# Two transformer blocks on one core: the first block's closing norm and the norm behind it from one pass of sums, and a feed-forward layer that starts before both

## The chip, the core and the metric

The kernel runs on one core of a Trainium2 chip. A core has five engines that run side by side, each through its own queue of instructions, in order, and that wait for one another on semaphores: PE (TensorE, matrix products into PSUM; the loading of its stationary operand is shown as PEld), DVE (VectorE), ACT (ScalarE), POOL (GpSimd, no access to PSUM) and SP, which here issues nearly all DMAs. The metric is the device time of one execution in microseconds.

## What is computed

The reference runs two stacked models on 256 tokens of width 1024, in float32. The first block ends with routed experts and a closing norm with the gain `g_final`; the second block takes that as its tokens `h`, beside a context `hc` of 256 tokens of its own, and begins with half of a feed-forward layer (FFN) on a norm that is scaled and shifted by a modulation.

```python
def first_block(...):
    ...
    x = x + _hier_moe(hm, ...).reshape(b, s, d)      # 32 experts, two per token
    return _rms_norm(x, g_final)                     # x / rms(x) * g_final

def _modulate(h, shift, scale):                      # rms norm without a gain, then scale and shift
    return _rms_norm_2(h) * (1.0 + scale) + shift

def second_block(x, c, ctx, ...):
    h, hc = x, ctx
    for layer in range(2):
        mod, modc = ...                              # from c and c_ctx: products with ada_w
        h = h + 0.5 * mod[:, 2] * _swiglu(_modulate(h, mod[:, 0], mod[:, 1]), ffn_w_in[layer, 0], ffn_w_out[layer, 0])
        hc = hc + ...                                # the same for the context
        ...                                          # a mixer, and a second FFN, for both
    return _rms_norm_2(h) * final_norm
```

## The kernel before

Activations lie feature-major: `xres` (the tokens) and `cres` (the context) are [128, 8, 256], eight chunks of 128 features by 256 tokens. Every fp32 product is made of three products of parts: a higher part `h` (a copy rounded by ACT to fp32r) and a lower part `l` (what is left, by DVE or POOL), for weights (`fsph`/`fspl` for tokens, `bsph`/`bspl` for the context, 128x512 each) and for activations (`fxh`/`fxl`, `bxh`/`bxl`). So 512 columns of weights are one ACT copy, one subtraction on DVE or POOL, and 12 matmuls with 256 columns.

Two streams are recorded: `fore` (names with f: first block, then the tokens of the second) and `back` (names with b: modulations and context). Within a stream each engine keeps the order in which the code emits; the two are merged by a priority (`seg`, a start and a slope), and a scheduler fixes one static order for each engine. Tile pools are small: three buffers each of `fsph`, `fspl`, `bsph`, `bspl` and of `fraw`, so a new part waits until PE is through with the part three before it. `Stream.low` chooses the engine of the lower parts: all of the context's go to POOL, the tokens' to DVE.

An FFN (`ffn_steps`) has 22 column blocks f: `gate_up(f)` makes the two products with 48 matmuls (gate and up), then tanh and products on ACT and DVE, and `down(r)` takes the finished blocks in rounds: 0 and 1, then four at a time.

`moe` (the routed experts) ends in a loop over left-over blocks; behind it comes the closing norm on the `fore` stream. `presum` squares the chunks (four ACT instructions 128x512) and adds them up on DVE (three adds 128x512, one 128x256); `stats` sums over features with matmuls by a column of ones; `newton` makes 1/rms on two columns with 12 small DVE instructions; `bcast` spreads it over all partitions (a DVE product with the identity, and a matmul by ones); eight DVE instructions then scale `xres` in place. `presum` runs again on the new `xres`, and `tokens()` begins with `modulated`, which is `stats`, `newton`, `bcast` and, per chunk, two DVE and one ACT instruction that make `fxh` and `fxl`. Only then the FFN's products can start. While this goes on, PE has matmuls of the context's FFN in its order.

The class `Ahead` is used by two later norms (layer 1): it splits g * res without the norm's factor (`step`), and the FFN's first two column blocks run on that, with the shift as two more columns (258 in place of 256). Meanwhile `factors` makes 1/rms; `norm` then makes the true `fxh` and `fxl` in the same place, `finish` completes the two early blocks, and the third block takes its weights in an order that follows the chunks. In these first blocks `EARLY_LOW` sends half of block 1's lower parts and all of block 2's to POOL. With `first`, four blocks instead of three come before `down(0)`, and one more ahead in the next round.

```python
            if f < early:                              # in gate_up, early = 2 with `first`
                p = [S.ps([128, 512])[:, :T + 2] for _ in range(2)]
            for s in range(2):
                self.proj_f(S, raw[s], KC, X, p[s])
                if f < early and s == 1 - f:
                    next(factors)
            ...
            if f == early - 1:
                first.norm()
                for i in range(early):
                    finish(i)
```

Of the kernel before, what the change touches and what calls it, by code (L numbers as in the profile page):

```python
# [15 lines left out]
OP = mybir.AluOpType  # L16
# [3 lines left out]
D = 1024  # L20
# [24 lines left out]
class Eng:  # L45
    """An engine whose instructions stay in the order in which the current chain emits them."""
# [23 lines left out]
class Stream:  # L70
# [11 lines left out]
    def seg(self, start, slope):  # L82
        """instructions from here on are due at start + slope * (matrix product time since here)"""
        self.start, self.slope, self.done = start, slope, 0.0
# [4 lines left out]
    def low(self, nc):  # L89
        """the engine of the next weights' lower parts"""  # L90
        self.lows += 1
        return nc.gpsimd if self.pool_low and self.lows % self.pool_low[1] < self.pool_low[0] else nc.vector
# [10 lines left out]
class Ahead:  # L103
    """a modulated norm whose reader starts without the norm's factors, on g * res and shift side by side"""
# [16 lines left out]
    def factors(self):  # L121
        """the factors token-major, and then what broadcasts them"""
# [9 lines left out]
    def norm(self):  # L132
        """the norm itself, in the same place"""
        nc = self.K.nc
        a = {}
        for c in range(KC + 1):
# [5 lines left out]
            if c > 0:  # L142
# [3 lines left out]
                                               op0=OP.add, op1=OP.subtract)  # L146


class Kern:
# [37 lines left out]
    def pair(self, S, src):  # L187
        """the two halves [128, 1024] of a unit"""
# [75 lines left out]
    def squares(self, S, res, d, one=False):  # L264
        """column blocks d and d + 1 of res are final: the squares for the norm that comes next, a step behind"""
# [18 lines left out]
    def presum(self, S, pairs):  # L284
        """the squares for the norm of what lies in pairs of chunks [128, 2, T]"""
# [33 lines left out]
    def head_rstd(self, S, y, eps):  # L319
        """1 / rms of each of the four chunks of y, as columns [128, (chunk, token block)]"""  # L320
# [22 lines left out]
    def gained(self, S, res, g, tag="k4"):  # L343
        """the parts of g * res, which lacks the norm's factors, and what makes those of one chunk"""
# [8 lines left out]
    def rstd_cols(self, S, st, n=D, eps=1e-6):  # L353
        """the norm's factors, token-major, from the sums of the squares"""
# [4 lines left out]
    def out_proj(self, S, src, X, res, gate, step=None):  # L359
        """res += gate * (X @ w), two column blocks per unit; step goes on with each final chunk"""  # L360
# [44 lines left out]
    def gated(self, S, src, n, out=None):  # L405
        """(tanh(src / 2) + 1) * src, twice the silu"""
# [12 lines left out]
    def ffn_steps(self, S, res, X, l, j, gate, first=None, then=None):  # L419
        """in steps of one round; first makes X, and then is what comes after it"""  # L420
# [8 lines left out]
        def product(f, a, b):  # L429
            """h = a * b"""  # L430
# [11 lines left out]
        def finish(f):  # L442
            """the rest of an early column block"""
# [84 lines left out]
    def ada(self, S, l, ms, tags):  # L528
        """the modulations ms of layer l, in steps of one load"""
# [24 lines left out]
    def logsig(self, S, z, shape):  # L554
        """log sigmoid of z, [128] + shape with 16 elements"""
# [23 lines left out]
    def narrow(self, S, src, n, m, tag="wg"):  # L579
        """the weights [128, KC * n] of n outputs, read in strips of m >= n columns"""  # L580
# [5 lines left out]
    def token_major(self, S, n, groups, passes):  # L586
        """the sums over the groups of k blocks, [128, 2, groups, n], of products with M = 128 / groups columns each"""
# [18 lines left out]
    def gates(self, S, w, n, X, bias, out, r=None):  # L606
        """out [128, 2, n] = r * (X @ w) + bias, token-major"""
# [7 lines left out]
    def doubled(self, S):  # L615
        """[128, 2, 72]: eight columns, and again from column 64 on"""
# [4 lines left out]
    def rows_hl(self, p, R):  # L621
        """the exact parts of eight rows: in R's rows 0 and 64 onwards"""
# [3 lines left out]
    def softmax(self, S, ps, nks, r=None):  # L626
        """softmax of the two query blocks of each p [128, 2, T], the first nks columns of which are keys;
        r are factors of the rows that p lacks"""
# [57 lines left out]
    def first_block(self, S):  # L686
# [37 lines left out]
        def queries(i):  # L724
            """keys and queries of a pair of heads: of the forgetting attention (i < 4) and of the differential one"""
# [17 lines left out]
        # forget gates  # L743
# [17 lines left out]
        # fox attention; keys and values of the memory  # L761
# [114 lines left out]
        # branches, gates and the output projection  # L876
# [40 lines left out]
        # cross attention  # L917
# [58 lines left out]
    def moe(self, S):  # L976
# [284 lines left out]
        if self.dbg:  # L1261
            self.dbg("x4", xres)
# [784 lines left out]
```

## Time and profile before

| | us |
|---|---|
| median of 3 runs | 2639.74 |
| lowest and highest run | 2637.49, 2642.59 |
| span of the profiled execution, first to last instruction | 2632.5 |
| PE busy in it | 2445.1 |

The profiled execution's own time is not listed beside its span; the median of the runs is 7.2 us above the span, and changes are worked out in the span and added to the median. A row that begins with a time is an instruction or a merged group: start, length, engine, line, operation, output and inputs, shapes, count, and in brackets the idle time just before it with what ended it.

### The profile page before, as it was taken

To read this page: it belongs to the slowest core of one execution; us is meant where nothing else is said; L and a number is where in the kernel's file an instruction comes from. 1 tells how busy PE (TensorE), PEld (TensorE's weight loads), DVE (VectorE), ACT (ScalarE), POOL (GpSimd) and SP (SyncE) were. 2 spreads that over 40 slices of the span, in tenths; PEclk is the share of its full clock that TensorE was granted. 3 is DMA by queue.
4 is the path that set the end of the run, shared out by engine and by line. 5 is a ranking of instruction groups with operands and counts; after the bars stand their busy time and mean duration, and the time that the engine had idled before them with its cause. 6 is when DMAs were issued, how large, how long until landed. Compare 5 with 4: busy or idle time off the path is not lost. (4 is left out here: it accounts for less than half of the span.)

```text
span 2632.5 us, 48460 instructions
## 1 busy us (share of the span) xinstructions
PE 2445.1 (93%) x19032; PEld 2073.7 (79%) x19032; DVE 1448.1 (55%) x3125; ACT 1186.9 (45%) x2342; POOL 730.4 (28%) x584
## 2 busy tenths in 40 slices
PE   6999998999988999999779999999999899888998
PEld 4767997785656787868359998876899899767998
DVE  6544767225433323332147676654766866676766
ACT  4433563334333433444125555543555555465554
POOL 1000145664424565656132004220100100333000
PEclk9999999999989999999779999999999999899999
DMA  9897443998988998989865553467555455312453
GB/s 346 325 317 247 171 142 112 357 329 296 364 317 336 350 347 296 366 324 345 321 250 175 186 189 125 164 202 269 195 175 182 154 184 185 112 65 97 161 186 119
DMA packets 117542, 617.37 MB, mean 235 GB/s; under 512 B 13488, under 2 KB 14960, under 8 KB 68288
## 3 DMA queue, kind: packets, MB, share of 16 engines
q1 hardware_dynamic: 115920, 610.20, 64.4%
q0 software_dynamic: 1392, 4.06, 0.5%
q8 instruction: 150, 2.46, 0.4%
q14 instruction: 80, 0.66, 0.1%
HBM read 612.11 MB, written 2.10 MB: 233 GB/s over the span
## 5 line engine op out<-in xcount | busy, mean ns | idle before, releaser
L58 POOL TENSOR_TENSOR bspl<-braw,bsph 128x512 fp32r<-128x512 f32 x468 | 608.9, 1308 | 947.6 <-ACT bsph L58 814.4
L58 ACT ACTIVATE fsph<-fraw 128x512 fp32r<-128x512 f32 x764 | 478.3, 628 | 540.3 <-PE fps L58 467.6
L58 DVE TENSOR_TENSOR fspl<-fraw,fsph 128x512 fp32r<-128x512 f32 x712 | 500.4, 706 | 309.2 <-ACT fsph L58 302.0
L58 PE MATMUL fps<-fxh,fspl 128*128 128x256 f32 (+1 forms) x2000 | 574.6, 287 | 3.9 <-POOL fspl L58 2.5
L58 PE MATMUL fps<-fxl,fsph 128*128 128x256 f32 (+1 forms) x2000 | 568.9, 284 | 8.8 <-DVE fxl L58 8.8
L58 PE MATMUL fps<-fxh,fsph 128*128 128x256 f32 (+1 forms) x2000 | 574.2, 287 | 3.1 <-ACT fsph L58 1.8
L58 ACT ACTIVATE bsph<-braw 128x512 fp32r<-128x512 f32 x468 | 291.7, 629 | 404.2 <-PE bps L58 350.4
L58 PEld LDWEIGHTS fps<-fxh,fspl 128*128 128x128 f32 x2000 | 381.8, 191 | 14.8 <-issue 5.8
L58 PEld LDWEIGHTS fps<-fxh,fsph 128*128 128x128 f32 x2000 | 383.3, 192 | 11.6 <-issue 4.8
L58 PEld LDWEIGHTS fps<-fxl,fsph 128*128 128x128 f32 x2000 | 382.7, 191 | 12.3 <-DVE fxl L58 11.3
L58 PE MATMUL bps<-bxh,bspl 128*128 128x256 f32 x1264 | 369.9, 293 | 2.1 <-ACT fk L58 2.1
L58 PE MATMUL bps<-bxh,bsph 128*128 128x256 f32 x1264 | 365.3, 289 | 5.5 <-ACT bsph L58 2.2
L58 PE MATMUL bps<-bxl,bsph 128*128 128x256 f32 x1264 | 362.4, 287 | 1.3 <-DVE bxl L58 1.3
L58 PE MATMUL fps<-fk,fsph 128*128 128x256 f32 x1632 | 299.3, 284 | 1.8 <-ACT fk L58 1.1
L58 PEld LDWEIGHTS bps<-bxh,bspl 128*128 128x128 f32 x1264 | 245.0, 194 | 53.1 <-POOL bspl L58 33.6
L58 PE MATMUL fps<-fraw,fk 128*32 128x512 f32 (+1 forms) x1600 | 234.9, 660 | 34.3 <-DMA fraw<-in_w_eu_dram 12.1
L58 PEld LDWEIGHTS bps<-bxh,bsph 128*128 128x128 f32 x1264 | 245.1, 194 | 26.5 <-issue 10.0
L58 PEld LDWEIGHTS fps<-fk,fsph 128*128 128x128 f32 x1632 | 254.8, 192 | 6.1 <-DVE fk L58 2.4
L58 PEld LDWEIGHTS bps<-bxl,bsph 128*128 128x128 f32 x1264 | 244.8, 194 | 17.6 <-issue 12.4
L58 POOL TENSOR_TENSOR fk<-fk,fk 128x512 f32<-128x512 f32 x16 | 21.6, 1349 | 761.9 <-ACT fk L58 756.8
L58 PE MATMUL fps<-fk,fspl 128*128 128x256 f32 x816 | 231.3, 283 | 0.0
L58 DVE SCALAR_TENSOR_TENSOR bk<-bk,bps 128x256 f32<-128x256 f32 (+1 forms) x148 | 60.5, 412 | 269.8 <-ACT bk L58 267.9
(353 smaller groups left out, 3482.3 us busy)
## 6 DMA issues: line engine op xcount, KB each, us to landing
fraw<-in_ffn_in_dram SPq DMA_DIRECT2D x88, 1024.0 KB, 4.9
braw<-in_ffn_in_dram SPq DMA_DIRECT2D x132, 512.0 KB, 6.2
fraw<-in_w_eg_dram SPq DMA_DIRECT2D x66, 1024.0 KB, 7.5
fraw<-in_w_eu_dram SPq DMA_DIRECT2D x66, 1024.0 KB, 7.3
fraw<-in_w_ed_dram SPq DMA_DIRECT2D x66, 1024.0 KB, 7.5
braw<-in_ada_w_dram SPq DMA_DIRECT2D x91, 512.0 KB, 6.1
fraw<-in_ffn_out_dram SPq DMA_DIRECT2D x44, 1024.0 KB, 4.9
braw<-in_ffn_out_dram SPq DMA_DIRECT2D x66, 512.0 KB, 5.6
```

Of the source, the lines that this page charges most:

```text
L58: r = f(*args, **kw)
```

## The change

`moe` no longer scales `xres` behind the loop. It makes the higher and lower parts of `xres * (g_final * scale)`, eight chunks, adds up the squares of `xres` as before, and a second sum of the squares of `g_final * xres` (eight ACT squares 128x256, the adds on POOL). The first FFN of the tokens takes the new `Ahead2` as `first`. From the two sums `factors` works out r1 (of the closing norm), then r of the norm behind it, with two Newton iterations one after the other, and two broadcasts. `norm` also scales `xres` itself, with eight DVE instructions behind the sixteen of the norm. What the diff leaves out are removed comments and docstrings.

```diff
+class Ahead2(Ahead):
+    def __init__(self, K, S, S2, res, g1, scale, shift):
+        super().__init__(K, S, S2, res, S.t("c", [128, KC]), shift)
+        self.g1, self.scale, self.all = g1, scale, res
+
+    def step(self, c):
+        if c == 0:
+            self.K.nc.vector.tensor_tensor(self.g, self.g1, self.scale, op=OP.mult)
+        super().step(c)
+
+    def factors(self):
+        K, S, nc = self.K, self.S, self.K.nc
+        st = self.S2.ps([128, 512])
+        for i, sq in enumerate(self.sq):
+            for b in range(2):
+                K.mm(st[:, 2 * i + b:2 * i + b + 1], sq[:, b * 128:(b + 1) * 128], K.ones[:, 0:1], True, True)
+        r1 = S.t("gc", [128, 2])
+        nc.vector.tensor_copy(r1, K.newton(S, st[:, 0:2], 2, 1.0 / D, 1e-6))
+        s2 = S.t("c", [128, 2])
+        nc.vector.tensor_tensor(s2, r1, r1, op=OP.mult)
+        nc.vector.tensor_tensor(s2, s2, st[:, 2:4], op=OP.mult)
+        r = K.newton(S, s2, 2, 1.0 / D, 1e-6)
+        nc.vector.tensor_tensor(r, r, r1, op=OP.mult)
+        yield
+        p = self.S2.ps([128, 512])
+        K.bcast(S, r, 2, p[:, :T])
+        K.bcast(S, r1, 2, p[:, T:])
+        self.bc = S.t("q1", [128, T])
+        self.b1 = S.t("q1", [128, T])
+        nc.scalar.activation(self.bc, p[:, :T], AF.Copy)
+        nc.scalar.activation(self.b1, p[:, T:], AF.Copy)
+        yield
+
+    def norm(self):
+        super().norm()
+        for c in range(KC):
+            self.K.nc.vector.scalar_tensor_tensor(self.res[c], self.res[c], self.g1[:, c:c + 1], self.b1,
+                                                  op0=OP.mult, op1=OP.mult)
...
         pairs = [xres[:, c:c + 2] for c in range(0, KC, 2)]
+        g4 = self.gains[:, 4]
+        a = self.first_ahead
+        for c in range(KC):
+            a.step(c)
         self.presum(S, pairs)
-        bc = self.rstd_bcast(S, [xres[:, c] for c in range(KC)], 1e-6)
-        for c in range(KC):
-            nc.vector.scalar_tensor_tensor(xres[:, c], xres[:, c], self.gains[:, 4, c:c + 1], bc,
-                                           op0=OP.mult, op1=OP.mult)
-        self.presum(S, pairs)
...
+        plain = S.sq[0]
+        gained = None
+        for c in range(0, KC, 2):
+            sq = S.t("k2", [128, 2, T])
+            for i in range(2):
+                nc.scalar.activation(sq[:, i], xres[:, c + i], AF.Square, scale=g4[:, c + i:c + i + 1])
+            if gained is None:
+                gained = sq
+            else:
+                nc.gpsimd.tensor_tensor(gained, gained, sq, op=OP.add)
+        nc.gpsimd.tensor_tensor(gained[:, 0], gained[:, 0], gained[:, 1], op=OP.add)
+        S.sq = None
+        a.sq = (plain, gained[:, 0])
...
         x = K.xres
-        X = K.modulated(fore, x, 0, 0, 0)
-        for _ in K.ffn_steps(fore, x, X, 0, 0, K.mods_col(0, 2, 0)):
+        for _ in K.ffn_steps(fore, x, None, 0, 0, K.mods_col(0, 2, 0), first=K.first_ahead):
             yield
...
     fore.seg(*SEG["route"])
+    K.first_ahead = Ahead2(K, fore, back, K.xres, K.gains[:, 4], K.mods_col(0, 1, 0), K.mods_col(0, 0, 0))
     K.moe(fore)
```

Until the end of the loop every engine's order is the same in both kernels. Behind it, ACT had these rows before (`fk<-xres` are the squares, `bsph` the context's weights, `fsph` the first weights of the tokens' FFN):

```order
L58 ACTIVATE fk_14238<-xres 128x512
L58 ACTIVATE fk_14241<-xres 128x512
L58 ACTIVATE fk_14244<-xres 128x512
L58 ACTIVATE bsph_14343<-braw_14292 128x512
L58 ACTIVATE bsph_14372<-braw_14367 128x512
L58 ACTIVATE bsph_14388<-braw_14367 128x512
L58 ACTIVATE fsph_14807<-fraw_14804 128x512
```

And it has these now, behind the copy of the shift:

```order
L58 ACTIVATE bsph_14339<-braw_14288 128x512
L58 ACTIVATE fxh_14238<-xres,fc_12036 128x256 x8
L58 ACTIVATE fk_14258<-xres 128x512
L58 ACTIVATE fk_14260<-xres 128x512
L58 ACTIVATE fk_14263<-xres 128x512
L58 ACTIVATE fk_14266<-xres 128x512
L58 ACTIVATE bsph_14368<-braw_14363 128x512
L58 ACTIVATE bsph_14384<-braw_14363 128x512
L58 ACTIVATE fsph_14748<-fraw_14744 128x512
L58 ACTIVATE fsph_14764<-fraw_14744 128x512
```

The eight chunks now stand ahead of the context's next weights and of `fsph_14748`. In PE's order 19 matmuls of the context lead, then two that read `bsph_14368`, then the first two of column block 0, which read `fsph_14748`; before, the sum of the squares followed the first nine, and block 0 came some 240 matmuls of the context later. All of block 0 now stands in front of those; the sums of the squares stand behind them, then half of block 1, then 22 of the context's, then the two broadcasts, then the rest of block 1.

On DVE, the end of the second Newton iteration and its broadcast read so before (`fc` are its columns, `fk<-consts` makes the broadcast's operand, `cres` is the context's update):

```order
L58 TENSOR_TENSOR fc_14753<-fc_14753,fc_14751 128x2
L58 SCALAR_TENSOR_TENSOR fc_14752<-fc_14753,fc_14752 128x2
L58 TENSOR_TENSOR fk_14767<-consts,fc_14752 128x256
L58 SCALAR_TENSOR_TENSOR bk_14593<-bk_14591,bps_14526 128x256
L58 SCALAR_TENSOR_TENSOR bk_14595<-bk_14593,bps_14526 128x256
L58 TENSOR_TENSOR bk_14597<-bk_14595,bk_14597 128x256
```

And so now:

```order
L58 TENSOR_TENSOR fc_14839<-fc_14839,fc_14837 128x2
L58 SCALAR_TENSOR_TENSOR cres<-bps_14713,mods,cres 128x256 x2
L58 SCALAR_TENSOR_TENSOR fc_14838<-fc_14839,fc_14838 128x2
L58 SCALAR_TENSOR_TENSOR fc_14839<-fc_14838 128x2
L58 TENSOR_TENSOR fc_14839<-fc_14839,fc_14837 128x2
L58 SCALAR_TENSOR_TENSOR fc_14838<-fc_14839,fc_14838 128x2
L58 TENSOR_TENSOR fc_14838<-fc_14838,fgc_14817 128x2
L58 TENSOR_TENSOR fk_14890<-consts,fc_14838 128x256
L58 TENSOR_TENSOR fk_14893<-consts,fgc_14817 128x256
```

The context's update stands inside the iteration, and what it reads, `bps_14713`, is finished by the last of the 22 matmuls that stand right in front of the broadcasts on PE.

Behind the norm DVE's order is now this (`xres<-xres,gains,fq` scales the residual, `fspl_15101` belongs to column block 3, the rest is `finish` of block 0); before, there was no such row between the norm and the next lower parts:

```order
L58 SCALAR_TENSOR_TENSOR xres<-xres,gains,fq_14897 128x256 x8
L58 TENSOR_SCALAR fc_14972<-fps_14746 128x1
L58 COPY fc_14972<-fps_14747 128x1
L58 SCALAR_TENSOR_TENSOR fk_14973<-fps_14746,fq_14896 128x256
L58 TENSOR_TENSOR fspl_15101<-fraw_15081,fsph_15100 128x512
L58 TENSOR_TENSOR fspl_15117<-fraw_15081,fsph_15116 128x512
```

The eight scalings stand ahead of the lower parts that block 3 needs. From the end of block 3 on PE's order is that of before (one column block fewer stands in the next round), up to the tokens' even mixer; from there to the next layer's first FFN the scheduler placed some of the context's matmuls and two loads of `ada_w` a little earlier.

## Rows read from the trace of the kernel before

**Rows 1.** The page: span, busy time, and PE's busy share and granted clock in 40 slices.
```profile
span 2632.5 us, 48460 instructions
PE 2445.1 (93%) x19032; PEld 2073.7 (79%) x19032; DVE 1448.1 (55%) x3125; ACT 1186.9 (45%) x2342; POOL 730.4 (28%) x584
...
PE   6999998999988999999779999999999899888998
...
PEclk9999999999989999999779999999999999899999
```
**Rows 2.** Stretches of time behind the loop: busy us of each engine, granted clock, DMA.
```profile
1350.50:1400.40 49.90, 43.14 (x303) 42.27 (x303) 42.85 (x81) 26.89 (x53) 30.31 (x23) 0.86 0.52 180
1400.40:1420.00 19.60, 19.60 (x166) 19.60 (x166) 14.25 (x30) 10.56 (x21) 2.44 (x2) 1.00 0.63 219
1420.00:1580.00 160.00, 160.00 (x1353) 160.00 (x1352) 112.16 (x210) 84.86 (x152) 0.00 (x0) 1.00 0.53 187
```
**Rows 3.** PE in order of time: all its waits between 1350 and 1400 us.
```profile
1352.62 0.39 PE L58 MATMUL bps<-bxh,bspl 128*128 128x256 f32 x1 [2.09 <-ACT fk L58]
...
1355.80 1.01 PE L58 MATMUL fps<-consts,fk 128*128 128x1 f32 x4 [1.66 <-DVE fk L58]
...
1367.11 0.70 PE L58 MATMUL fps<-fk,consts 128*128 128x256 f32 x2 [0.82 <-DVE fk L58]
...
1378.61 0.95 PE L58 MATMUL fps<-consts,fk 128*128 128x1 f32 x4 [2.19 <-DVE fk L58]
```
**Rows 4.** Stretches of 1 us where the granted clock (third from the end) changes.
```profile
1354.00:1355.00 1.00, 0.14 (x2) 0.00 (x0) 0.97 (x2) 0.62 (x2) 1.00 (x1) 0.91 1.11 467
...
1360.00:1361.00 1.00, 1.00 (x7) 1.00 (x6) 1.00 (x2) 0.00 (x0) 1.00 (x1) 0.50 1.03 422
1361.00:1362.00 1.00, 1.00 (x8) 1.00 (x7) 1.00 (x5) 0.41 (x1) 0.14 (x1) 0.68 1.01 414
...
1378.00:1379.00 1.00, 0.39 (x3) 0.39 (x3) 0.89 (x3) 0.08 (x1) 0.00 (x0) 0.86 0.44 111
...
1385.00:1386.00 1.00, 1.00 (x8) 1.00 (x8) 0.70 (x2) 0.24 (x1) 0.96 (x1) 0.73 0.71 225
```
**Rows 5.** ACT in order of time, behind the loop and at a later norm of this kind.
```profile
1350.87 2.19 ACT L58 ACTIVATE fk<-xres 128x512 f32<-128x512 f32 x4 [7.14 <-PEq L1245]
1352.97 1.66 ACT L58 ACTIVATE bsph<-braw 128x512 fp32r<-128x512 f32 x3
...
2055.57 0.91 ACT L58 ACTIVATE fxh<-xres,mods 128x256 fp32r<-128x256 f32 x2
```
**Rows 6.** POOL, and DVE's small instructions of a Newton iteration beside it, in order of time.
```profile
1382.49 1.27 POOL L58 TENSOR_TENSOR bspl<-braw,bsph 128x512 fp32r<-128x512 f32 x1 [1.28 <-ACT bsph L58]
...
1382.25 0.16 DVE L58 SCALAR_TENSOR_TENSOR fc<-fc,fc 128x2 f32<-128x2 f32 x1
1382.45 0.16 DVE L58 SCALAR_TENSOR_TENSOR fc<-fc 128x2 f32<-128x2 f32 x1
1382.64 1.14 DVE L58 TENSOR_TENSOR fc<-fc,fc 128x2 f32<-128x2 f32 x1
```
**Rows 7.** PE in order of time at the later norm: sum of squares, and broadcast.
```profile
2070.34 0.50 PE L58 MATMUL bps<-consts,fk 128*128 128x1 f32 x4
...
2076.31 0.70 PE L58 MATMUL bps<-fk,consts 128*128 128x256 f32 x2 [2.46 <-DVE fk L58]
```
**Rows 8.** The stretch from that broadcast until the early blocks are finished.
```profile
2076.30:2100.00 23.70, 20.00 (x148) 18.50 (x149) 20.25 (x43) 13.88 (x30) 4.32 (x3) 1.00 0.35 125
```
**Rows 9.** DVE in order of time: the scaling of xres, and an update of the context.
```profile
1367.84 3.23 DVE L58 SCALAR_TENSOR_TENSOR xres<-xres,gains,fps 128x256 f32<-128x256 f32 x8 [0.46 <-PE fps L58]
...
1388.61 0.86 DVE L58 SCALAR_TENSOR_TENSOR cres<-bps,mods,cres 128x256 f32<-128x256 f32 x2
```
**Rows 10.** PE's waits from 1400 us to the end: total us, times, longest.
```profile
PE bps L58 <- DMA braw<-in_ada_w_dram: 13.0, 10, 2.3
```

More of the change, by code (lines that the diff above doesn't have):

```diff
@@ L1254, in moe @@
         pairs = [xres[:, c:c + 2] for c in range(0, KC, 2)]
+        g4 = self.gains[:, 4]
+        a = self.first_ahead
+        for c in range(KC):
+            a.step(c)
         self.presum(S, pairs)
-        bc = self.rstd_bcast(S, [xres[:, c] for c in range(KC)], 1e-6)
-        for c in range(KC):
-            nc.vector.scalar_tensor_tensor(xres[:, c], xres[:, c], self.gains[:, 4, c:c + 1], bc,
-                                           op0=OP.mult, op1=OP.mult)
-        self.presum(S, pairs)
-        if self.dbg:
-            self.dbg("x4", xres)
+        plain = S.sq[0]
[11 more added lines that the diff above has]
+        a.sq = (plain, gained[:, 0])
     def conv_silu(self, S, p, n, scale, out):
```

## The prediction

> **What bounds the kernel now.** The page comes first: PE is busy 2445.1 of 2632.5 us and its slices read 9 nearly everywhere, except at the start, in slices 20 and 21 (about 1250 to 1380 us), where the granted clock falls too, and in some later slices [rows 1]. The change works at the end of that dip, so I went on to stretches of time. From 1350.5 us, the end of the expert loop, to 1400.4 us PE is busy 43.14 of 49.90 us; behind that it is busy all the time until 1580 us [rows 2]. So whatever PE loses between 1350.5 and 1400.4 is lost for good, and whatever the change wins or loses there should reach the end as it is.
>
> PE loses in two ways there. The first is idle time, 49.90 - 43.14 = 6.76 us, and PE's own list shows it all: 2.09 us at the loop's exit, 1.66 before the first sum of squares, 0.82 before the first broadcast, 2.19 before the second sum [rows 3]. The rest of both norms is already covered by the context's matmuls. The second is the clock: it falls to 0.5 (1.2 GHz) late in the microsecond from 1354 and is back at 1361.7, and again from 1378.9 to 1385.6 [rows 4]; at full clock PE starts 1353 matmuls in 160 us, one every 0.118 us [rows 2], and at half the clock each takes twice that. PE is at work in some 5.8 us of the first stretch and 6.7 of the second, and half of that is lost: 6.2 us. Together 13.0 us, of which 2.1, the exit, stays in any case.
>
> **What the change does to PE's own work.** Almost nothing. There are two sums of squares and two broadcasts as before; 96 matmuls get 258 columns in place of 256, 96 x 0.118 x 2/256 = 0.1 us. Column block 3 only changes places with the first round's `down`. Everything hangs on waits. I lay the new order out from the loop's exit, with durations from the rows, and add up what PE loses until the end of block 3.
>
> **First wait: the chunks stand ahead of the weights on ACT.** ACT begins at 1350.87. The copy of the shift is small (0.3 as an estimate, below the 0.4 of a chunk); one 128x512 copy takes 0.52 (1.66 for three, whose last tail is 0.1), a scaled chunk 0.41 (0.91 for two), four squares 2.1 [rows 5]. So `bsph_14368` is ready at 1350.87 + 0.3 + 0.52 + 8 x 0.41 + 2.1 + 0.6 = 1357.7, and `fsph_14748` one copy later and one more, at about 1358.75. PE starts at 1352.62 as before [rows 3], has 19 matmuls (2.3 us) and then must wait from 1354.9, with 0.25 us of work on the way: **3.6 us**. It is 2.5 if a chunk takes only half of a square, 0.27 (8 x 0.14 = 1.1 less), and 3.9 if the first chunk waits 0.3 for DVE's product of the two gains.
>
> **POOL and DVE behind it.** Four adds for the second sum (3 x 1.3 and 0.7 us) now stand on POOL between the context's lower parts, 1.27 us each. Rows 6 show what that does to DVE: an instruction of 0.16 us that starts while POOL is at work takes 1.14 us and ends when POOL ends. DVE has the adds of squares, `fspl_14749` and the context's products there, and ACT's `fsph_14796` stands behind a copy that waits for such a product. It costs nothing if DVE slips between, and one and a half POOL instructions, 2.0, if not; I take **0.9**.
>
> **The clock.** PE is idle for 2.1 us, works for 2.3 and is idle again for 3.6. Before, 4.4 us with 1.4 of work came ahead of the first fall, and an idle time of 2.19 us ahead of the second [rows 3, 4]. A fall costs at most what it did, 3.3; none costs 0. I take **2.5**, nearer to the fall, since the idle time is longer here than at either place.
>
> Up to here (block 0 and some 45 of the context's matmuls) PE has lost 9.1 us, where it lost 2.1 + 1.66 + 0.82 + 2.9 = 7.5 before. From there the context's matmuls run without the wait of 2.19 and the fall of 3.3.
>
> **Second wait: the factors.** The sums stand some 190 matmuls later. Behind them PE has 24 matmuls of block 1 and 22 of the context's, 5.5 us, then the broadcasts. DVE needs 13 small instructions (0.195 from start to start) [rows 6], two products, 13 more, one product and the operand of the broadcast (0.43). Inside stands the update of `cres`, which needs the last of PE's 22 matmuls; so, however fast DVE is, PE waits for 0.3 us until that product has landed, 0.86 for the update [rows 9], four small instructions and a product (1.0) and 0.43: at least 2.5 us. At most: the five POOL subtractions that fall into this stretch each hold an instruction back by 1.0 us, as in rows 6, and a sixth the broadcast's, so that the chain ends 12.0 us behind the sums and PE waits 5.8. The nearest row, one iteration at the later norm, took 5.97 us from sum to broadcast, and PE waited 2.46 with 24 fewer small steps to wait for [rows 7]. I take the middle, **4.2**.
>
> Here the Trainium skill bears on the sum: its page "SBUF — State Buffer", section "Who interferes with whom", says that a DVE instruction with two SBUF inputs and a GpSimd instruction that reads SBUF exclude each other for the whole instruction, and that the order of issue decides who blocks. Our rows show such waits, 1.14 for 0.16 us, but not at every overlap: the row at 1382.45 has one input and runs on. Taken as strictly as the page states it, this wait would be 5.8 and the whole sum 1.6 us more than mine.
>
> **Third wait: the norm, and the scaling of xres.** From the broadcast on the program is that of the later norm, where PE lost 23.70 - 20.00 = 3.7 us until the early blocks were finished [rows 8]; I take **3.7**, between 2.9 (without the longest POOL delay) and 4.5. New is the scaling of `xres` on DVE between the norm and block 3's lower parts and `finish`: 3.23 us [rows 9]. At the later norm PE already waits there, so little is left to hide it: 0 if it is hidden, 3.2 if not, taken **2.7**. A second fall of the clock, behind the wait for the factors, would cost block 1's last 24 matmuls 2.3 us, mostly hidden by the norm: **0.3**.
>
> **The sum.** After: 2.1 + 3.6 + 0.9 + 2.5 + 4.2 + 3.7 + 2.7 + 0.3 = 20.0 us lost, before 13.0: **7.0 us more**. All lower ends give 10.0 (3.0 us less), all upper ones 27.1 (14.1 more). SP's queue has the same DMAs; one load of the tokens moves ahead of four of the context's, whose buffers come free later anyway. The span would be 2639.5 us, the median 2639.7 + 7.0 = **2646.7 us**. 0.2% is 5.3 us, about what this measurement can tell from no change.
>
> **The rivals.**
> 1. *Waits of the same size, no change.* DVE slips between POOL's instructions and the clock holds: 2.1 + 3.6 + 0.2 + 0.5 + 2.6 + 3.7 + 1.2 = 13.9, 0.9 more, 2640.6 us. For it: the second iteration of before took 4.3 us in spite of POOL, and the later norm had no fall. Against it: 3.6 us of idle time at the first wait is fixed by ACT's order, and the five POOL instructions by PE's.
> 2. *DVE is held at each step.* The factors take 12 us, the clock falls twice, `xres` is not hidden: 5.8 + 3.2 + 2.3 and the other upper ends, 10 to 14 more, about 2651.5 us. For it: rows 6. Against it: what the norm hides.
> 3. *Not slower, by the loads of `ada_w`.* PE waits 13.0 us in ten pieces for these loads further on, the longest 2.3 [rows 10]. Two of them now stand earlier. If each takes one such wait with it, 4.6 are won: 2.4 more remain, 2642.1 us, no change; from one wait (1.7 us) on the result is inside 0.2%, and it takes six of them for a gain. Against it: loads that stand earlier only shift the wait where the DMA queue is the bound.
>
> **Chances.** The forecast (3 to 10 more) 0.45; rival 1 0.28; rival 2 0.15; rival 3 0.12. Slower by over 0.2%: two thirds of the forecast's and all of rival 2, 0.46. Within 0.2%: the rest of the forecast, most of rivals 1 and 3, 0.41. Faster: the ends of rivals 1 and 3, in which the order further on wins several us, 0.13. The range leaves out 1 in 10 on either side: from 4.0 us less (all lower ends and 1 us further on) to 15.3 more (all upper ends and 1): 2636 to 2655. The forecast's own is 2642.7 to 2649.7.
>
> **What would show it.** Right: PE idle for about 3 us and then 0.8 us before its first 258-column matmul, near 1355 to 1359; no waits of PE from there to the sums near 1394; an idle time of 2.5 to 6 us in front of the broadcasts; column block 3 with a wait for `fspl` of about 2 us, and its end near 1427 instead of 1420. Wrong: if the clock stays at 1.0 from 1350 to 1430, or the broadcasts wait below 2 us, the loss shrinks to rival 1; if PE shows the same loss up to block 3 and the end comes elsewhere, the order further on decided it.

## The result: 0.64% slower

| | before | changed |
|---|---|---|
| median, us | 2637.07 (7 runs, 2629.24 to 2642.59) | 2652.28 (7 runs, 2643.78 to 2657.14) |
| span of the profiled execution | 2632.5 | 2650.5 |
| ratio to before, 95% interval | | 1.0064 (1.0045 to 1.0083) |

The forecast was slower, 2646.7 us, with a range up to 2655; the time lies in the range and on the forecast's side, 5.6 us above its likeliest value. The change itself is larger than that sounds: the forecast added 7.0 us to a median of three runs (2639.74), and with seven runs the median of before is 2637.07, so the medians are 15.2 us apart, twice the forecast and as much as its upper end (15.3). The ratio's interval is 12 to 22 us.

The page of the changed kernel has the same dip in slices 20 to 22 (compare [rows 1]):

```profile
span 2650.5 us, 48502 instructions
...
PE 2457.1 (93%) x19032; PEld 2077.4 (78%) x19032; DVE 1450.2 (55%) x3137; ACT 1192.1 (45%) x2359; POOL 742.1 (28%) x594
...
PE   6999998999989999999778999999999999888998
...
PEclk9999999999999999999689999999999999899999
```

Both kernels have 19032 matmuls, so stretches of equal work can be cut by counting them. I cut one from PE's first matmul behind the loop (to within 0.2 us of its start) over 635 matmuls (column blocks 0 to 3 and the context's work between them lie in it) and one over the next 1181. A row gives the ends and the length, the busy time of PE, PEld, DVE, ACT and POOL, then the granted clock, the DMA share and GB/s. Of before:

```profile
1352.62:1440.02 87.40, 82.73 (x635) 81.89 (x636) 70.67 (x136) 46.80 (x90) 32.76 (x24) 0.92 0.54 192
1440.02:1580.07 140.05, 140.05 (x1183) 140.05 (x1182) 98.10 (x183) 73.76 (x132) 0.00 (x0) 1.00 0.54 188
```

And of the changed kernel, with the rest of the span as a third row:

```profile
1353.36:1452.97 99.61, 85.78 (x636) 82.41 (x637) 73.45 (x146) 52.94 (x106) 44.92 (x34) 0.93 0.47 168
1452.97:1594.42 141.45, 141.45 (x1183) 141.45 (x1182) 98.40 (x183) 73.71 (x133) 0.00 (x0) 1.00 0.53 186
1594.42:2650.50 1056.08, 982.77 (x7726) 907.46 (x7725) 715.49 (x1487) 540.13 (x1058) 161.97 (x131) 0.96 0.46 160
```

The 18.0 us between the two spans are 0.7 that were there before the change's first instruction (1353.36 - 1352.62), **12.2 in the stretch of the change** (99.61 - 87.40), **1.4 in the next**, in which PE is never idle in either kernel, and 3.7 behind it. In the first stretch PE is idle for 99.61 - 85.78 = 13.8 us in place of 4.7; the low clock takes as much of it as before (0.93 of 99.61 and 0.92 of 87.40 are both some 14 us at half the clock). PE's waits there over 0.15 us, in order of time, with the sums (1395.66) among them:

```profile
1353.29 0.39 PE L58 MATMUL bps<-bxh,bspl 128*128 128x256 f32 x1 [2.15 <-ACT fxh L58]
...
1358.06 0.39 PE L58 MATMUL bps<-bxh,bsph 128*128 128x256 f32 x1 [2.25 <-ACT bsph L58]
...
1359.10 0.58 PE L58 MATMUL fps<-fxh,fsph 128*128 128x258 f32 x1 [0.54 <-ACT fsph L58]
...
1363.08 0.39 PE L58 MATMUL fps<-fxh,fspl 128*128 128x258 f32 x1 [0.78 <-DVE fspl L58]
...
1369.02 0.39 PE L58 MATMUL fps<-fxh,fsph 128*128 128x258 f32 x1 [1.08 <-ACT fsph L58]
...
1370.48 0.39 PE L58 MATMUL fps<-fxh,fspl 128*128 128x258 f32 x1 [0.36 <-DVE fspl L58]
...
1395.66 0.95 PE L58 MATMUL bps<-consts,fk 128*128 128x1 f32 x8
...
1407.70 2.08 PE L58 MATMUL bps<-fk,consts 128*128 128x256 f32 x4 [5.50 <-DVE fk L58]
...
1418.00 0.39 PE L58 MATMUL fps<-fxh,fsph 128*128 128x256 f32 x1 [0.17 <-ACT fsph L58]
...
1419.65 0.39 PE L58 MATMUL fps<-fxh,fspl 128*128 128x256 f32 x1 [1.14 <-POOL fspl L58]
...
1424.65 0.36 PE L58 MATMUL fps<-fxh,fsph 128*128 128x256 f32 x1 [0.97 <-DVE fk L58]
...
1431.81 0.88 PE L58 MATMUL fps<-fk,fsph 128*128 128x256 f32 x2 [0.84 <-ACT fk L58]
```

The 2.19 us in front of the second sum are gone (the row at 1395.66 has no wait), and 5.50 stand before the broadcasts in their place. Most waits also cost something that is no idle time: the first matmul behind one takes 0.39 us and not 0.28, and the next starts as much later.

What DVE did between the sums and the broadcasts, with POOL beside it:

```profile
1396.25 1.28 POOL L58 TENSOR_TENSOR bspl<-braw,bsph 128x512 fp32r<-128x512 f32 x1
...
1398.77 2.75 POOL L58 TENSOR_TENSOR fspl<-fraw,fsph 128x512 fp32r<-128x512 f32 x2 [1.24 <-ACT fsph L58]
1401.47 2.68 POOL L58 TENSOR_TENSOR bspl<-braw,bsph 128x512 fp32r<-128x512 f32 x2
...
1396.64 0.16 DVE L58 TENSOR_SCALAR fc<-bps 128x2 f32<-128x2 f32 x1 [0.15 <-PE bps L58]
1396.84 0.72 DVE L58 TENSOR_SCALAR fc<-fc 128x2 int32<-128x2 int32 x1
...
1398.97 1.14 DVE L58 SCALAR_TENSOR_TENSOR fc<-fc 128x2 f32<-128x2 f32 x1
...
1400.34 1.20 DVE L58 SCALAR_TENSOR_TENSOR fc<-fc,fc 128x2 f32<-128x2 f32 x1
1401.57 1.22 DVE L58 COPY fgc<-fc 128x2 f32<-128x2 f32 x1
...
1403.21 0.95 DVE L58 TENSOR_SCALAR fc<-fc 128x2 f32<-128x2 f32 x1
...
1407.57 0.42 DVE L58 TENSOR_TENSOR fk<-consts,fgc 128x256 f32<-128x256 f32 x1
```

The line from the first small instruction to the second operand takes 11.4 us. Five instructions in it that take 0.16 to 0.17 elsewhere last 0.72 to 1.22, each until a POOL instruction is done; together that is 4.4 us. Two of the five are `TENSOR_SCALAR` and one a `COPY`, with one input each. Behind the broadcasts the clock is low as well, although PE works without a break: the rows are two stretches of the changed kernel at half the clock.

```profile
1408.00:1413.00 5.00, 5.00 (x20) 4.64 (x20) 2.53 (x6) 2.39 (x6) 0.11 (x1) 0.50 0.00 0
1420.00:1423.00 3.00, 3.00 (x17) 3.00 (x16) 3.00 (x8) 0.00 (x0) 0.00 (x0) 0.50 0.71 243
```

### The profile page after: what moved, and what is told of

Its sections match the earlier page's. It is cut to its first block, busy times and chain, and to the rows that moved or that the text cites. A ratio compares the mean times of both kernels' runs of the same rounds, so it can differ in the third digit from the quotient of the medians.

```text
span 2650.5 us, 48502 instructions
## 1 busy us (share of the span) xinstructions
PE 2457.1 (93%) x19032; PEld 2077.4 (78%) x19032; DVE 1450.2 (55%) x3137; ACT 1192.1 (45%) x2359; POOL 742.1 (28%) x594
## 5 line engine op out<-in xcount | busy, mean ns | idle before, releaser
L58 PEld LDWEIGHTS fps<-fxh,fsph 128*128 128x128 f32 x2000 | 386.8, 193 | 13.8 <-issue 5.0
```

What stands on the lines that cost most here:

```text
L58: r = f(*args, **kw)
```

## The experiments

All are measured against the kernel before. The first three columns of numbers behind the ratio are of the same 635 matmuls as above, the last of the 1181 behind them; each is one profiled execution. In it the low clock comes and goes with the execution (0.90 to 0.96 in these stretches), so idle time tells more than length.

| kernel | ratio (95% interval) | stretch, us | PE idle | granted clock | next 1181 matmuls, us |
|---|---|---|---|---|---|
| before | | 87.40 | 4.7 | 0.92 | 140.05 |
| changed | 1.0064 (1.0045 to 1.0083) | 99.61 | 13.8 | 0.93 | 141.45 |
| 1 sums in the tokens' PSUM | 1.0068 (1.0052 to 1.0085) | 98.64 | 12.3 | 0.91 | 141.45 |
| 2 xres scaled later | 1.0075 (1.0060 to 1.0089) | 100.12 | 14.2 | 0.93 | 141.46 |
| 3 both | 1.0051 (1.0038 to 1.0064) | 96.51 | 13.3 | 0.96 | 141.45 |
| 4 the tokens' work off POOL | 1.0056 (1.0037 to 1.0076) | 95.98 | 12.0 | 0.95 | 141.46 |
| 5 shared sums alone | 1.0072 (1.0051 to 1.0093) | 101.11 | 15.3 | 0.90 | 140.04 |
| 6 early start alone | 1.0021 (1.0005 to 1.0037) | 92.54 | 10.2 | 0.96 | 141.45 |
| 7 changed, chunks 256 apart | 1.0071 (1.0049 to 1.0092) | 100.62 | 16.0 | 0.95 | 140.04 |
| 8 before, chunks 256 apart | 0.9997 (0.9979 to 1.0015) | 85.97 | 4.7 | 0.94 | 140.04 |
| 9 shared sums, own PSUM | 1.0031 (1.0014 to 1.0047) | 93.28 | 9.5 | 0.93 | 140.04 |
| 10 changed, own PSUM | 1.0042 (1.0023 to 1.0061) | 92.83 | 10.5 | 0.96 | 141.43 |
| 11 as 9, chunks 256 apart | 1.0030 (1.0014 to 1.0046) | 93.27 | 9.6 | 0.93 | 140.04 |
| 12 early start, own PSUM for the sums, 256 apart | 1.0018 (1.0003 to 1.0034) | 93.43 | 8.4 | 0.91 | 140.29 |

**Experiment 1.** Why do the sums stand 190 matmuls late? Their tile comes from `S2`, the context's stream, whose PSUM pool has three buffers, and so has to wait for the context's tiles ahead of it in the ring.

```diff
 def factors(self):
-        st = self.S2.ps([128, 512])
+        st = S.ps([128, 512])
```

> One word is changed against the changed kernel: the tile of the four column sums is taken from the tokens' own PSUM pool and no longer from the context's, so that on PE the sums stand right behind column block 0 and some 190 matmuls of the context stand between them and the broadcasts. Theory F (the largest part of the loss is that the sums stand late, so that the two Newton iterations are not covered: a wait of 5.5 us before the broadcasts and a low clock behind it that costs 2.7): the wait is gone, the clock stays up there, and the time falls by 8 to 10 us, to about 2643. Theory S (the loss is DVE's work behind the broadcasts: norm, scaling of xres, lower parts): the wait goes, but PE waits as long behind the broadcasts, and the time falls by less than 3 us, to about 2650. Theory L (the loss comes from the order further on and from the clock there): no change, 2652.

Measured: 1.0068, no gain. The wait of 5.5 is gone as theory F says, and three others are there:

```profile
1390.44 0.39 PE L58 MATMUL bps<-bxh,bsph 128*128 128x256 f32 x1 [2.06 <-ACT bsph L58]
...
1391.81 0.39 PE L58 MATMUL bps<-bxh,bspl 128*128 128x256 f32 x1 [0.86 <-POOL bspl L58]
...
1421.07 0.58 PE L58 MATMUL fps<-fxh,fsph 128*128 128x256 f32 x1 [3.15 <-ACT fsph L58]
```

And ACT's row ahead of the first of them:

```profile
1389.45 0.42 ACT L58 ACTIVATE bk<-bk 128x256 fp32r<-128x256 f32 x1 [4.77 <-DVE bk L58]
```

The two iterations now stand on DVE in front of the context's products; ACT stands 4.77 us behind such a product, and the context's next weights behind ACT. Later `fsph` of column block 2 stands on ACT behind the chunks of the norm, which DVE delivers. As these rows read, the wait follows whatever stands behind DVE's line. Theory F falls as an account of the whole; S is nearest.

**Experiment 2.** The eight scalings of `xres` behind column block 3.

```diff
 class Ahead2
-    def norm(self):
-        super().norm()
+    def scale_res(self):
         for c in range(KC):
 gate_up, behind product(f, ...)
+            if f == 3 and hasattr(first, "scale_res"):
+                first.scale_res()
```

> The eight scalings of xres on DVE stand behind column block 3's products and no longer between the norm and finish; all else, PE's order too, is that of the changed kernel. Theory S: PE's waits for finish and for block 3's lower parts (0.97 and about 1 us) and the low clock before them (1.7) shrink, 2 to 4 us less, about 2649. Theory F: only what is left of these waits, at most 1.5 us less, about 2651. Rival: the scalings only move, and hold up the products of block 3 instead: no change, 2652.

Measured: 1.0075, 14.2 us of idle time against 13.8: nothing won. The wait of 0.97 for `finish` goes, and about as much stands in front of the next `down` and behind it. The rival's "no change" came out. The times alone could not tell the 2 to 4 us of theory S from nothing; it is the idle time that speaks against "the scaling is in the wrong place".

**Experiment 3.** Both edits.

> The sums in the tokens' own PSUM pool and the scalings behind block 3, together. Theory F with S: the gains add up, 10 to 13 us less than the changed kernel, about 2640, and within 0.2% of the kernel before. If both remove the same wait, no more than the better of the two alone, about 2643. Theory L: no change, 2652.

Measured: 1.0051, with an interval that meets those of 1, of 2 and of the changed kernel. Idle time is 13.3 us; the shorter stretch is the granted clock, 0.96. The 10 to 13 us of F with S did not come.

**Experiment 4.** The adds of the second sum and the lower parts of column blocks 1 and 2 on DVE.

```diff
-                nc.gpsimd.tensor_tensor(gained, gained, sq, op=OP.add)
+                nc.vector.tensor_tensor(gained, gained, sq, op=OP.add)
 ...
-                S.pool_low = EARLY_LOW[f] if f < len(EARLY_LOW) else LOW[S.name]
+                S.pool_low = EARLY_LOW[f] if f < len(EARLY_LOW) and not hasattr(first, "sq") else LOW[S.name]
```

> The adds of the second sum and the lower parts of column blocks 1 and 2 go from POOL to DVE; the order on PE stays. Theory P (POOL's instructions, which hold up DVE's for about 1 us each, are what makes the wait for the factors and those for lower parts long): the wait of 5.5 before the broadcasts shrinks by about 2 us, the one of 1.1 for a lower part from POOL goes, 2 to 4 us less, about 2649. Rival: DVE is short of time there, and what it takes over (four adds and six subtractions, about 7 us) comes back as waits of PE: 1 to 4 us more, about 2655.

Measured: 1.0056, not to be told from 1.0064. In the trace theory P is half right: the wait before the broadcasts is 4.0 in place of 5.5, the one for POOL's lower part is gone, and the stretch is 3.6 us shorter; a wait of 2.6 for DVE's `finish`, 0.97 before, stands where DVE took over. The context's lower parts are still on POOL here.

**Experiments 5 and 6.** The two halves of the change. In the first, no chunk is made ahead, and the FFN begins behind a norm from the shared sums:

```diff
-        for c in range(KC):
-            a.step(c)
         self.presum(S, pairs)
 ...
-        for _ in K.ffn_steps(fore, x, None, 0, 0, K.mods_col(0, 2, 0), first=K.first_ahead):
 ...
+        f = a.factors()
+        next(f)
+        next(f)
+        a.norm()
+        for _ in K.ffn_steps(fore, x, a.X, 0, 0, K.mods_col(0, 2, 0)):
```

> Half of the change alone: one pass of sums for both norms, and the FFN begins behind the norm, on tiles of 256 columns. Theory Q (the loss is DVE's: the two iterations, the norm and the scaling stand in one line with too little of the context's work behind them, so PE waits some 5.5 us before the broadcasts wherever the FFN begins): slower than before by 6 to 12 us, PE waits about 5.5 before the broadcasts and 3 or more behind them. Theory E (the early start of the FFN is what costs: its chunks and first weights on ACT, its restarts, its wider tiles): as before or faster, within 3 us of it.

In the second the closing norm has its own pass of sums, and the existing class `Ahead` starts the FFN early (the lines of the second sum, left out here, go too):

```diff
+        self.presum(S, pairs)
+        bc = self.rstd_bcast(S, [xres[:, c] for c in range(KC)], 1e-6)
         for c in range(KC):
-            a.step(c)
+            nc.vector.scalar_tensor_tensor(xres[:, c], xres[:, c], self.gains[:, 4, c:c + 1], bc,
+                                           op0=OP.mult, op1=OP.mult)
+        for c in range(KC):
+            self.first_ahead.step(c)
         self.presum(S, pairs)
 ...
-    K.first_ahead = Ahead2(K, fore, back, K.xres, K.gains[:, 4], K.mods_col(0, 1, 0), K.mods_col(0, 0, 0))
+    K.first_ahead = Ahead(K, fore, back, K.xres, K.mods_col(0, 1, 0), K.mods_col(0, 0, 0))
```

> The other half alone: the closing norm with its own pass of sums as before, then the early start on chunks without the second norm's factor, as at the later norms. Theory E: slower than before by 6 us or more, with PE's waits in block 0 and a wait of 2 to 3 us before the broadcast. Theory Q: the factors are one iteration, so the wait before the broadcast is 2 to 3 us in place of 5.5, and the whole is slower than before by 2 to 5 us, of which 2 are the wider tiles.

Measured: **1.0072 for the shared sums alone, 1.0021 for the early start alone**. The shared sums alone cost as much as the whole change. The two halves make 0.93% together against its 0.64%, which the intervals do not tell apart. What PE waited for with the shared sums alone (total, times, longest, over the stretch):

```profile
PE bps L58 <- DVE fk L58: 6.4, 1, 6.4
PE bps L58 <- POOL bspl L58: 4.0, 3, 1.7
PE fps L58 <- DVE fspl L58: 3.3, 1, 3.3
```

and with the early start alone:

```profile
PE fps L58 <- DVE fk L58: 3.0, 3, 1.6
PE bps L58 <- DVE fk L58: 2.5, 1, 2.5
```

One iteration is waited for 2.5 us, two in a row 6.4. E fails at the first. Q's waits came out in both, but its time for the first did not: it gave 6 to 12 us, and 0.72% is 19. Part of that is a wait that nobody forecast, the 4.0 us for `bspl`: PE stood 1.7 and 1.0 us for lower parts of the context that came behind adds of the second sum on POOL.

**Experiments 7 and 8.** In the changed kernel PE takes 141.45 us for what took 140.05, without one idle moment, in the second stretch. The tiles of an early FFN have 258 columns for each chunk, so the true chunks lie 258 apart for all later blocks too. The edit writes them 256 apart in the same tile; every engine's order stays.

```diff
-            xh, xl = (S.t(tag, [128, KC, T + 2], F32R) for tag in ("xh", "xl"))
+            self.flat = [S.t(tag, [128, KC * (T + 2)], F32R) for tag in ("xh", "xl")]
+            xh, xl = (t.rearrange("p (k t) -> p k t", k=KC) for t in self.flat)
 ...
-                a[c], h = self.S.t("k1", [128, T]), self.X.h[c][:, :T]
+                a[c], h = self.S.t("k1", [128, T]), self.flat[0][:, c * T:(c + 1) * T]
 ...
-                l = self.X.l[d] = self.X.l[d][:, :T]
+                l = self.X.l[d] = self.flat[1][:, d * T:(d + 1) * T]
```

> The changed kernel, but norm writes the true parts of the chunks 256 columns apart and not 258, in the same tiles; every engine's order is the same. It holds for the three FFNs that begin early (one in layer 0, two in layer 1). Theory T (behind the first two blocks PE's matmuls on these tiles start every 119.7 ns and not every 117.8 since the chunks lie 258 columns apart): 117.8 in all three, 20 blocks x 48 x 0.0019 = 1.9 us each, 5.6 less in all, about 2646. Rival (the rate is set by the weights or the clock, not by where the chunks lie): 119.7 stays, no change, 2652.

> The kernel before with the same edit, which reaches its two early FFNs in layer 1. Theory T: 117.8 there too, 3.7 us less than before (0.14%). Rival: no change.

The row of the second stretch in the changed kernel with this edit:

```profile
1460.24:1600.28 140.04, 140.04 (x1183) 140.04 (x1182) 97.95 (x183) 73.88 (x132) 0.00 (x0) 1.00 0.53 187
```

Theory T holds in the trace: 140.04 again. The mean distance of two starts among the matmuls on these tiles goes from 119.7 to 117.8 ns here, and in before from 119.7 to 117.9 and 118.5 in the FFNs of layer 1 (some 930 to 950 distances each, without waits and low clock). The whole time doesn't show it: 1.0071 and 0.9997, where 5.6 and 3.7 us were expected; the second, 0.14%, is inside its interval, the first (1.0043) just below it. In the changed kernel the wait for DVE in front of column block 3 was 2.50 in place of 0.97 and took part of it back.

**Experiment 9.** The shared sums alone, the tiles of the sums and of the broadcasts from the tokens' PSUM pool.

```diff
-        st = self.S2.ps([128, 512])
+        st = S.ps([128, 512])
 ...
-        p = self.S2.ps([128, 512])
+        p = S.ps([128, 512])
```

> The half with the shared sums alone, as before, but the tiles of the four column sums and of the two broadcasts come from the tokens' PSUM pool. On PE the sums then stand behind some 9 and 70 of the context's matmuls, 85 more stand between them and the first broadcast, and 24 between the broadcasts and block 0. Theory R (what makes the shared sums dear is that their tiles wait in the ring of the context's PSUM pool, so that everything behind them stands in one line at its end): PE's idle time in the stretch falls from 15 us to below 6, and the time is that of the kernel before, within 3 us. Theory Q (DVE's longer line of small instructions itself): 8 us or more of idle time stay, and it is slower than before by 0.4% or more.

Measured: 1.0031, idle 9.5 us against 15.3 of experiment 5 (1.0072, intervals apart). The time lies between the two theories; the idle time is Q's (8 or more). The edit takes over half of the loss away. Of the idle time, some 3 us less are waits for the context's lower parts from POOL and 2.4 the wait before the broadcast, where PE still stands 3.99 us; that rest is Q. DVE's rows of the two iterations, and POOL's idle time:

```profile
1370.07 0.16 DVE L58 TENSOR_SCALAR fc<-fps 128x2 f32<-128x2 f32 x1 [3.27 <-PE fps L58]
...
1373.89 1.21 DVE L58 SCALAR_TENSOR_TENSOR fc<-fc,fc 128x2 f32<-128x2 f32 x1
1375.14 1.22 DVE L58 SCALAR_TENSOR_TENSOR fc<-fc 128x2 f32<-128x2 f32 x1
...
1379.83 0.17 DVE L58 COPY fgc<-fc 128x2 f32<-128x2 f32 x1
...
1380.42 0.57 DVE L58 TENSOR_SCALAR fc<-fc 128x2 f32<-128x2 f32 x3
...
1383.06 0.16 DVE L58 SCALAR_TENSOR_TENSOR fc<-fc,fc 128x2 f32<-128x2 f32 x1
...
1384.00 2.75 POOL L58 TENSOR_TENSOR bspl<-braw,bsph 128x512 fp32r<-128x512 f32 x2 [4.81 <-ACT bsph L58]
```

The same twelve instructions take 9.8 us beside POOL (1370.07 to 1379.83; POOL works until 1379.2) and 2.8 us while POOL is idle (1380.42 to 1383.22), with three and two products of the context among them. This is the clearest pair of rows on what POOL does to such a line.

**Experiment 10.** The same two words in the whole changed kernel.

> The whole change with both kinds of tiles from the tokens' PSUM pool, the broadcasts too. On PE some 80 of the context's matmuls stand between the sums and the broadcasts, and 110 behind the broadcasts. Theory R: the wait of 5.5 and the waits behind the broadcasts that the first of these experiments showed in its place both shrink, the idle time in the stretch falls from 12 to 14 us to below 9, and it is slower than before by 0.2 to 0.4%, the rest being the first waits and the wider tiles. Theory Q: the waits only move once more, and it is slower by 0.6% or more.

Measured: 1.0042, idle 10.5 us; the wait before the broadcasts is 2.8, and column block 2 no longer waits for its weights. Its median, 2643.39 (8 runs), is 11.9 above that of before (2631.53) where the changed kernel's was 15.2 above its own. Neither theory came out whole: R gave 0.2 to 0.4% and idle time below 9, Q 0.6% or more. The interval meets that of the changed kernel, so the times alone don't show a gain; the idle time, 10.5 against 13.8, does.

**Experiments 11 and 12.** Two candidates for a version that wins. The first is experiment 9 with the true chunks of layer 1's early FFNs 256 apart, the second the early start alone with the sums in the tokens' PSUM pool and chunks 256 apart:

```diff
-        r = K.newton(self.S, K.stats(self.S, self.res, self.S2)[:, 0:2], 2, 1.0 / D, 1e-6)
+        r = K.newton(self.S, K.stats(self.S, self.res)[:, 0:2], 2, 1.0 / D, 1e-6)
```

> The shared sums alone with their tiles in the tokens' PSUM pool, and with the true chunks of the two early FFNs in layer 1 256 columns apart. Theories R and T together: 3 to 4 us less than the same kernel without that spacing, so 0 to 6 us less than the kernel before. If R fails: slower than before by 0.3% or more.

> The early start alone (the closing norm with its own pass of sums), with the column sums of the three early FFNs in the tokens' PSUM pool and the true chunks 256 columns apart. Theories R and T: the longest wait of the early start alone, 2.5 us, shrinks and the three FFNs take 1.9 us less each, so it is 3 to 8 us less than the early start alone was: from 0.1% faster than the kernel before to 0.05% slower. If the wait only moves to what stands behind DVE's line: 0.05 to 0.2% slower.

Measured: 1.0030 and 1.0018. Neither beats the kernel before: 11 was expected 0 to 6 us below it and met the sign that R fails (0.3% or more), and of 12 the rival came out. The spacing is not seen in either time, though 117.9 to 118.6 ns are seen in the traces. In the second the wait of 2.5 for the broadcast went and came back as in experiment 1:

```profile
PE fps L58 <- ACT fsph L58: 3.2, 1, 3.2
```

## Why it came out so

The mechanism of the forecast was right: PE is the bound, no work of its own goes away, and the change turns covered norms into waits. Its sizes were off, mostly to the low side: the change lies outside the forecast's own 3 to 10 us, and that the time is inside the whole range is owed to the upper end and in part to luck, since the median of before came out 2.7 lower with more runs. What PE lost, by the forecast's terms (idle time from the rows; the clock is what matmuls took longer in stretches at half the clock, about; late starts are the rest, 635 x 0.1182 = 75.1 us being PE's time for the stretch without any):

| | forecast | trace |
|---|---|---|
| exit of the loop | 2.1 | 2.2 |
| first wait, ACT's order | 3.6 | 2.8 (2.25 + 0.54) |
| POOL and DVE behind it | 0.9 | 2.2 (0.78 + 1.08 + 0.36) |
| clock there | 2.5 | 1.5 |
| wait for the factors | 4.2 | 5.5 |
| clock behind it | 0.3 | 3.1 |
| norm, scaling, finish | 3.7 + 2.7 | 3.4 idle, 1.6 clock |
| late starts | none | 4.4 |
| sum | 20.0 | 26.7 |
| same sum for before | 13.0 | 14.4 (1.7 late starts) |

- **First wait.** The step held: `bsph_14368` was forecast for 1357.7 and PE went on at 1358.06. PE waited 2.8 us in place of 3.6: it began 0.7 later, the weights came 0.4 later, and its matmuls ahead of them took some 0.5 longer than booked. Behind it PE waited three times in block 0 for ACT and DVE, 2.2 us; the upper end, one and a half POOL instructions (2.0), was nearer than the 0.9 taken, and the sign "no waits from there to the sums" did not come.
- **The wait for the factors** was 1.3 us longer than booked. The forecast gave bounds of 2.5 and 5.8 and took the middle; from the first of the sums to the broadcasts 12.0 us passed (1395.66 to 1407.70), as at the upper end. The row that spoke for the middle was misread: the instruction at 1382.45 in [rows 6] has one name behind the arrow because it reads the same tile twice, and it ran on because POOL's began 0.04 us later. The strict reading gave 5.8, and 5.5 came. Experiment 9 agrees with it: 9.8 us beside POOL, 2.8 without. It is the rule of the Trainium skill, "SBUF — State Buffer", section "Who interferes with whom": a DVE instruction with two SBUF inputs and a GpSimd instruction that reads SBUF contend, and whoever issues first blocks the other.
- **The clock behind that wait** was, with 2.8 us, the booked term most below its size: it was put at 0.3, as hidden by the norm. It was not hidden: PE was busy through 1408 to 1413 at half the clock, and went on from column block 1 into block 2 without a wait for the norm that could have hidden it. In all, the low clock took what it took before (6.2 and 6.0 us). The forecast's "twice" for a matmul at half the clock is too much: 13 starts from 1420.17 to 1422.73 of the changed kernel lie 0.213 us apart, 1.8 times the 0.118.
- **Late starts** were put at nothing. Twelve waits in place of three (the smallest 0.1 us) cost 2.7 us more than their idle time.
- **The scaling of `xres`** was booked at 2.7. With the norm and `finish` it came to 5.0 in place of 6.4. Moving it (experiment 2) won no idle time; that PE waits for DVE's line wherever it stands is a reading of that, not a test of its own.
- **PE's own work** was put at 0.1 for 96 wider matmuls. The rows show 1.4 us in the second stretch alone, since the other blocks read chunks 258 columns apart; experiment 7 takes them away by the spacing alone.
- **Rival 3**, a gain further on by the loads of `ada_w`, did not come: PE waits 12.1 us for them in place of 13.0 [rows 10]. Behind 1594 us the changed kernel lost 3.7 more; over the twelve experiments this part was between 4.4 less and 5.0 more than in the one execution of before, so it is not put down to the order.
- **Rival 2** (DVE held at each step, 10 to 14 more), given a chance of 0.15, is nearest to what happened, in mechanism and size: 12.3 us up to the end of the first stretch. Column block 3 ended at 1430.5, where 1427 was forecast, without its wait for `fspl`.

What the forecast did not see is why the sums stood late. It took the order as given. The tiles of the sums and of the broadcasts stood in the ring of the context's PSUM pool; experiments 5 and 9 show that with both moved the shared sums cost 0.31% in place of 0.72%. Moved for the sums alone (1 and 12), the wait comes back one step later. What is left in 9 and 10 is mainly the wait for DVE's two iterations (3.99 and 2.8 us); in 9 the first of them, beside POOL, takes most of it. Whether the context's lower parts could be kept off POOL in that stretch was not tried, so how much of the rest is POOL's is open.

## What to carry to other kernels

A norm that PE's other work already covers costs little (4.7 us of idle time for two here); merging two of them saves DVE time that PE hardly waited for (66.3 us busy in the stretch of experiment 5, 70.7 before) and makes one chain twice as long, and it is the chain that has to be covered. Before moving a wait, look at what stands behind it on the same engine: in four of these kernels (1, 2, 3 and 12) the named wait went and most of the time came back at a later instruction. A tile that is widened for a few instructions is read by all later ones: look at the spacing of the matmuls behind it as well.

## What was not expected of the hardware

PE's matmuls with 256 columns start every 117.8 to 118.5 ns on average when the moving chunks lie 256 fp32 columns apart, and every 119.7 ns at 258 apart, with the same instructions in the same order (experiments 7 and 8); no cause was tested. In the second stretch of the changed kernel the chunks 1, 3 and 5 of a block take 121.7 to 123.0 ns and the others 117.5 to 118.8, 104 to 108 distances each. Chunks 1, 3 and 5 start at odd multiples of 1032 bytes, but so does chunk 7, which takes 117.5, so the start alone doesn't explain it. The granted clock can be low behind a wait although PE works without a break from its end: 1408 to 1413 us at 0.50 behind 5.5 us of idle time.
